# Three input loads of a dilated convolution, each in two transfers of half the rows

## The chip, the cores and the metric

The kernel runs on one core of a Trainium2 chip. The metric is the device time of one execution in microseconds. Beside it stands a profile of one execution, whose span reaches from the first instruction to the last.

## What is computed

A 3x3 convolution with dilation 2 and zero padding of 2, in float32, on 16 images of 64 channels and 64x64 points, with 128 output channels:

```python
batch, c_in, h, w, c_out, k, dilation = 16, 64, 64, 64, 128, 3, 2
...
x_pad = np.pad(x, ((0, 0), (0, 0), (pad, pad), (pad, pad)), mode='constant')
...
output[b, co] += weight[co, ci, kh, kw] * x_pad[b, ci, kh*dilation:kh*dilation+h, kw*dilation:kw*dilation+w]
```

The input has 16.8 MB and the output 33.6 MB.

## The kernel before

**Tiles.** Two images make a pair: their 2 x 64 channels fill the 128 partitions, so that one pair of input is 128 rows of 16 KB in HBM, one for each partition. There are eight pairs (`NP`), numbered from 0; the sixth to eighth are pairs 5, 6 and 7. A pair's output is a tile `o` of 128 partitions (output channels) by two images of 16 KB each, 4 MB in all.

**Arithmetic.** Input is held in float16 (`x16`, six buffers). Rows that stand two apart share part of their work: GpSimd (POOL in the profile) adds them to `s16` (three buffers, `prepare`, line 141), TensorE (PE) multiplies the sums once with the middle row of the weights (`w1`), and two more phases use differences of weight rows (`w21`, `w01`) and the outer rows. For each of four stretches `u` of 16 image rows, ScalarE (ACT) copies the first phase from PSUM to `s32` (line 204), and VectorE (DVE) adds it to the other two and writes `o` (line 209). The matmuls of the two images of a pair, 64 partitions each, are issued in turn (line 186).

**Loads.** Pair 0 comes as float32 by two transfers of SyncE's queue (SP, line 75), 36 and 28 rows, and is cast on chip. Pairs 1 to 7 come by `load` (lines 78 to 81): GpSimd issues the transfers, and they cast from float32 to float16 on the way. `load(pb, cuts)` makes one transfer for each stretch of rows between two neighbours in `cuts`. Pair 1 is issued among the preparation of the weights, pairs 2 to 4 after the first sum of pair 0 (`AHEAD` is 5). Pairs 5, 6 and 7 are issued in the main loop (line 196), at `u == 1` of pairs 3, 4 and 5, each ahead of `prepare` of the pair after that one (lines 199 and 201: rows 0 to 35, then the rest).

**What sets the order.** The schedule is by hand: each engine works off its instructions in the program's order and waits where it needs a result or a free buffer. GpSimd has little to do, so it runs ahead in the program until it needs a buffer: `prepare` of pair 4 waits for PE to be done with the `s16` of pair 1, and so on. So the loads of pairs 5 to 7 are issued long before PE comes to the place where they stand. The buffers of pairs 6 and 7 are those of pairs 0 and 1.

**Stores.** SP issues one store of 4 MB after each of pairs 0 to 4 (line 221), two of 2 MB (one per image) after pairs 5 and 6, and for pair 7 two of 1 MB after each half of its rows (line 224). Tile `o` has three buffers. Loads of GpSimd run in queue q0, all transfers of SP in queue q1; both are served by the same 16 DMA engines. A transfer over 128 partitions puts 8 partitions on each engine. A packet is one stretch of memory of one partition, 16 KB for a whole input row or one image of a store; each engine ends its part of a transfer with a small semaphore packet of 4 bytes.

Of the kernel before, what the change touches and what calls it, by code (L numbers as in the profile page):

```python
# [10 lines left out]
def kernel(  # L11
# [9 lines left out]
    B, CI, H, W = x.shape  # L21
# [56 lines left out]
    def load(pb, cuts):  # L78
        x16[pb] = x16pool.tile([P, H, W], f16, tag="x16", name=f"x16_{pb}")
        for lo, hi in zip(cuts, cuts[1:]):  # L80
            nc.gpsimd.dma_start(out=x16[pb][:, lo:hi], in_=x_pair[pb, :, lo:hi])  # L81
# [53 lines left out]
    def prepare(pb, lo, hi):  # L135
        if pb not in s16:
            s16[pb] = sumpool.tile([P, 2 * NQ, W], f16, tag="s16", name=f"s16_{pb}")
        src = (x16[pb] if pb else x32).rearrange("p (q e r) w -> p q e (r w)", e=2, r=2)
        dst = s16[pb].rearrange("p (q r) w -> p q (r w)", r=2)
        q0, q1 = lo // 4, hi // 4  # L140
        nc.gpsimd.tensor_add(  # L141
            out=dst[:, q0:q1], in0=src[:, q0:q1, 0, :], in1=src[:, q0:q1, 1, :]
        )
# [37 lines left out]
    def phase(pb, u, terms):  # L181

        ps = cpool.tile([CO, 2, NB], f32, tag="ps", name="ps")
        for pair in zip(*(conv(pb, hb, ps[:, hb], u, terms) for hb in range(2))):
            for m in pair:
                nc.tensor.matmul(**m)  # L186
        return ps

    BOTH = NP - 3
    for pb in range(NP):  # L190
        o = opool.tile([P, 2, H, W], f32, tag="o", name=f"o{pb}")
        ov = o.rearrange("p b (q e r) w -> p b q e (r w)", e=2, r=2)
        for u in range(NU):

            if u == 1 and AHEAD <= pb + 2 < NP:
                load(pb + 2, [0, H])
            if pb + 1 < NP:
                if u == 1:
                    prepare(pb + 1, 0, 36)
                elif u == 2:  # L200
                    prepare(pb + 1, 36, H)

            s32 = spool.tile([P, 2, NB], f32, tag="s32", name="s32")
            nc.scalar.copy(out=s32, in_=phase(pb, u, [("w1", 2, 0)]))  # L204
            for e, terms in enumerate(
                ([("w21", 1, 0), ("w0", 1, -1)], [("w01", 0, 0), ("w2", 0, 1)])
            ):
                ps = phase(pb, u, terms)
                nc.vector.tensor_add(  # L209
                    out=ov[:, :, u * UQ : (u + 1) * UQ, e, :],  # L210
                    in0=ps.rearrange("p b (q c) -> p b q c", c=QW),
                    in1=s32.rearrange("p b (q c) -> p b q c", c=QW),
                )

            step = NU // 2 if pb == NP - 1 else NU
            if (u + 1) % step == 0:
                fl = slice((u + 1 - step) * 4 * UQ, (u + 1) * 4 * UQ)
                if pb < BOTH:  # L220
                    nc.sync.dma_start(out=out_pair[pb], in_=o)
                else:
                    for hb in range(2):
                        nc.sync.dma_start(out=out[2 * pb + hb, :, fl], in_=o[:, hb, fl])
# [35 lines left out]
```

## Time and profile before

| what | value |
|---|---|
| median of 3 runs | 126.64 us (126.33 to 126.74) |
| profiled execution: span of its instructions | 124.3 us |
| busy: PE, DVE, POOL, ACT | 105.2, 80.8, 41.4, 39.6 us |
| read from and written to HBM | 17.07 and 33.55 MB, 407 GB/s over the span |
| queue q1 (SP: weights, pair 0, all stores) | 2944 packets, 68.9% of 16 engines' span |
| queue q0 (POOL: loads of pairs 1 to 7) | 1008 packets, 28.4% |
| load of one pair, issue to landing | 16.0 us in the median of 7 |
| store of 4 MB, issue to landing | 21.6 us in the median of 5 |

The profiled execution has no time of its own beside its span. Busy times are unions of an engine's instructions. In the table of 40 slices each digit is the busy share of one fortieth of the span in tenths, 9 for 90% or more; the DMA row is the mean over the 16 DMA engines, and the GB/s row counts what packets wrote, so a load that casts counts with half of what it read. The share of a queue is the time of its packets over 16 engines' time; since records of neighbouring packets overlap a little, the shares of a full stretch come to slightly over 100%. In a timeline row stand the start and the length of a run of like instructions, and in square brackets how long the engine was idle ahead of it and what ended that.

### The profile page before, as it was taken

What the parts mean: (1) busy time and instruction counts of PE and PEld (TensorE: products, weight loads), DVE (VectorE), ACT (ScalarE), POOL (GpSimd) and SP (SyncE); (2) the same over time, 40 slices, a digit from 0 to 9 for tenths busy, and PEclk for the clock granted to TensorE, in tenths of its full rate; (3) what the DMA queues carried; (4) which work ended last, traced back from release to release, by engine and by line L of the source; (5) the groups of instructions that cost most, each with busy time, mean ns of one, the idle gap of its engine ahead of it and who ended that gap; (6) DMA issues with size and microseconds to landing.
All of it is one profiled execution on the core that took longest, in us unless ns stands there. A gap on an engine that the chain in (4) does not pass through costs nothing.

```text
span 124.3 us, 2244 instructions
## 1 busy us (share of the span) xinstructions
PE 105.2 (85%) x981; PEld 55.7 (45%) x981; DVE 80.8 (65%) x71; ACT 39.6 (32%) x40; POOL 41.4 (33%) x33
## 2 busy tenths in 40 slices
PE   6357999999999999999999999999999999960000
PEld 2043555555555555555555555555555555520000
DVE  0470199787778777877769778777877787770000
ACT  4760823333333333333333333333332433320000
POOL 2859998794095009500930093000000000000000
PEclk9999999999999999999999999999999999999655
DMA  4999999999999999999999999999999999999991
GB/s 129 346 359 218 214 214 216 224 237 411 393 327 314 332 306 319 316 390 314 324 345 427 425 427 432 422 427 427 432 438 427 432 414 432 427 417 419 422 406 71
DMA packets 3961, 43.42 MB, mean 349 GB/s; under 512 B 368, under 2 KB 368, under 8 KB 624
## 3 DMA queue, kind: packets, MB, share of 16 engines
q1 hardware_dynamic: 2944, 35.95, 68.9%
q0 software_dynamic: 1008, 7.34, 28.4%
q8 instruction: 7, 0.11, 0.3%
q14 instruction: 2, 0.02, 0.0%
HBM read 17.07 MB, written 33.55 MB: 407 GB/s over the span
## 4 chain that ended last, share of the span: by engine, by line
PE 80%; DMA 5%; POOL 2%; DVE 1%; DVEq 1%; SPq 0%; issue 0%
PE ps L186 80%; DMA x<-in_x_dram 5%; POOL s L141 2%; DVE o L209 1%; DVEq L255 1%; SPq L64 0%; DVEq L209 0%
## 5 line engine op out<-in xcount | busy, mean ns | idle before, releaser
L209 DVE TENSOR_TENSOR o<-ps,s 128x1024 f32<-128x1024 f32 x64 | 76.7, 1223 | 25.9 <-PE ps L186 16.8
L186 PE MATMUL ps<-x,w_sb 64*128 64x496 f16 (+3 forms) x768 | 85.3, 368 | 0.0
L186 PEld LDWEIGHTS <-w_sb 64*128 64x128 f16 x960 | 53.4, 95 | 49.3 <-issue 3.7
L204 ACT COPY s<-ps 128x1024 f32<-128x1024 f32 x32 | 32.4, 1012 | 63.0 <-PE ps L186 63.0
L141 POOL TENSOR_TENSOR s<-x 128x1152 f16<-128x1152 f16 (+4 forms) x18 | 35.1, 1971 | 31.1 <-PE ps L186 28.3
L186 PE MATMUL ps<-s,w_sb 64*128 64x496 f16 (+1 forms) x192 | 26.5, 379 | 2.1 <-POOL s L141 2.1
L81 POOL DMA_DIRECT2D x<-in_x_dram x7 | 4.0, 579 | 0.0
L132 ACT CAST x<-x 128x1024 f16<-128x1024 f32 (+1 forms) x3 | 2.8, 973 | 3.4 <-DMA x<-in_x_dram 3.4
L93 PE MATMUL warm<-zero 128*128 128x512 f16 x6 | 2.7, 630 | 1.2 <-DVE zero L87 1.2
L117 PE MATMUL wt<-ident,w 128*128 128x128 f16 x15 | 1.8, 312 | 2.1 <-ACT w L99 2.1
L103 DVE TENSOR_TENSOR w<-w 128x192 f16<-128x192 f32 x2 | 1.5, 800 | 2.5 <-DMA w<-in_weight_dram 2.5
L117 PEld LDWEIGHTS <-w 128*128 128x128 f16 x15 | 1.5, 146 | 3.0 <-ACT w L99 3.0
L99 ACT CAST w<-w 128x576 f16<-128x576 f32 x2 | 2.3, 1222 | 1.6 <-DMA w<-in_weight_dram 1.6
L103 POOL TENSOR_TENSOR w<-w 128x192 f16<-128x192 f32 x2 | 1.9, 951 | 2.4 <-DMA w<-in_weight_dram 2.4
L126 DVE CAST w_sb<-wt 128x384 f16<-128x384 f32 x3 | 1.6, 552 | 1.4 <-PE wt L117 1.4
L93 PEld LDWEIGHTS <-zero 128*128 128x128 f16 x6 | 0.7, 138 | 2.3 <-DVE zero L87 1.2
L99 ACT ACT_TABLE_LOAD x1 | 1.3, 1283 | 0.7 <-PEq L241 0.7
L128 ACT CAST w_sb<-wt 128x384 f16<-128x384 f32 x2 | 1.0, 478 | 1.1 <-PE wt L117 1.1
L130 DVE CAST x<-x 128x1280 f16<-128x1280 f32 x1 | 0.8, 826 | 0.5 <-DMA x<-in_x_dram 0.5
L87 DVE MEMSET zero<- 128x256 uint32 x1 | 0.3, 272 | 0.9 <-PEq L241 0.9
masks.py:199 POOL TENSOR_SCALAR_AFFINE_SELECT ident<-ident 128x128 f16<-128x128 f16 x1 | 0.3, 292 | 0.1
masks.py:197 POOL MEMSET ident<- 128x128 f16 x1 | 0.2, 204 | 0.3 <-POOLq L241 0.3
(4 smaller groups left out, 0.4 us busy)
## 6 DMA issues: line engine op xcount, KB each, us to landing
out_dram<-o SPq DMA_DIRECT2D x5, 4096.0 KB, 21.6
out_dram<-o SPq DMA_DIRECT2D x4, 2048.0 KB, 12.4
x<-in_x_dram POOLq DMA_DIRECT2D x7, 1024.0 KB, 16.0
out_dram<-o SPq DMA_DIRECT2D x4, 1024.0 KB, 10.6
x<-in_x_dram SPq DMA_DIRECT2D x1, 1152.0 KB, 6.5
x<-in_x_dram SPq DMA_DIRECT2D x1, 896.0 KB, 10.6
w<-in_weight_dram SPq DMA_DIRECT2D x1, 288.0 KB, 2.9
```

Source lines behind the costliest of these rows:

```text
L81: nc.gpsimd.dma_start(out=x16[pb][:, lo:hi], in_=x_pair[pb, :, lo:hi])
L93: nc.tensor.matmul(out=warm[:, 0], lhsT=zero[:, 0:P], rhs=zero, start=True, stop=True)
L99: nc.scalar.copy(out=w16[:, 0:NK, u, :], in_=w32k)
L103: eng.tensor_sub(out=w16[:, SLOT[name] * KW : (SLOT[name] + 1) * KW, u, :], in0=w32k[:, a * KW : (a + 1) * KW, :], in1=w32k[:, KW : 2 * KW ...
L117: nc.tensor.matmul(out=ps[:, 0, j * CO : (j + 1) * CO], lhsT=w16[:, k0 + j, :, :].rearrange("o t i -> o (t i)"), rhs=ident, start=True, st ...
L126: nc.vector.tensor_copy(out=dst, in_=ps[:, 0, 0 : KW * CO])
L132: nc.scalar.copy(out=x16[0][:, lo:hi], in_=x32[:, lo:hi])
L141: nc.gpsimd.tensor_add(out=dst[:, q0:q1], in0=src[:, q0:q1, 0, :], in1=src[:, q0:q1, 1, :])
L186: nc.tensor.matmul(**m)
L204: nc.scalar.copy(out=s32, in_=phase(pb, u, [("w1", 2, 0)]))
L209: nc.vector.tensor_add(out=ov[:, :, u * UQ : (u + 1) * UQ, e, :], in0=ps.rearrange("p b (q c) -> p b q c", c=QW), in1=s32.rearrange("p b ( ...
L255: with _tile.TileContext(nc) as tc:
```

## The change

Where the loads of pairs 5, 6 and 7 are issued, the list of cuts gets 32 as a middle point, so each load becomes two transfers, of rows 0 to 31 and of rows 32 to 63. Each is still one stretch per partition, of 8 KB instead of 16 KB in HBM, and of 4 KB instead of 8 KB on chip. The tile, the casting and the place in the program stay. The loads of pairs 0 to 4 and all stores are as before.

```diff
             if u == 1 and AHEAD <= pb + 2 < NP:
-                load(pb + 2, [0, H])
+                load(pb + 2, [0, 32, H])
             if pb + 1 < NP:
                 if u == 1:
                     prepare(pb + 1, 0, 36)
```

## The prediction

> **What bounds the kernel now.** I read the page's slices first, then the chain of work, then the DMA view of single stretches, and last the packet records in order of their start.
>
> ```profile
> PE   6357999999999999999999999999999999960000
> ...
> DMA  4999999999999999999999999999999999999991
> GB/s 129 346 359 218 214 214 216 224 237 411 393 327 314 332 306 319 316 390 314 324 345 427 425 427 432 422 427 427 432 438 427 432 414 432 427 417 419 422 406 71
> ```
>
> The DMA engines are full from the second slice to the last but one. PE stops in the 36th slice, and three slices of nothing but transfers follow. GB/s counts a cast load by what it writes, half of what it reads, so the lower numbers in slices 4 to 9 and 12 to 21 are loads, not idle engines.
>
> ```profile
> PE ps L186 80%; DMA x<-in_x_dram 5%; POOL s L141 2%; DVE o L209 1%; DVEq L255 1%; SPq L64 0%; DVEq L209 0%
> ...
> 110.88 1.13 DVEq L255
> ```
>
> The chain names PE for 80% and ends at 112.0 us, 12 us before the span's end. It follows instructions; the rest of the span is the queue of transfers that it does not walk. The packet records show that queue: the last data packets end between 120.5 us on the engine done first and 122.9 us on the engine done last. PE's last matmul is at 110.3 us and the last store is issued at 112.4 us, while that store's first packet starts at 118.0 us. So the store had to wait for the queue, and **the end is the sum of all packets on the latest engine**; a cost on PE, DVE, ACT or POOL shows only when it makes that queue run empty.
>
> Does the sum close? On the engine done first, the fourth load's semaphore packet is at 27.68 us and its last at 120.54 us: 92.86 us. Five stores of 4 MB at 9.72 us, four of 2 MB at 4.86 and four of 1 MB at 2.455 make 77.9, three loads at 4.87 make 14.6, together 92.5 (the durations are distances between such packets of transfers that follow each other with nothing between). 0.36 us is left over, in the 24 places where loads and stores alternate.
>
> **The change, part by part.** The loads of pairs 5, 6 and 7 (image rows 0 to 31, then 32 to 63) become six transfers. Nothing else is edited.
>
> *Packets.* Each engine moves 8 partitions of a pair, in 8 packets of 16 KB read and 8 KB written. It will have 16 packets of 8 KB read and 4 KB written: 24 more packets per engine in all. The trace has no cast packet of that size. The nearest rows are stores of the two sizes:
>
> ```profile
> DMA packets 157, 2.57 MB, mean 429 GB/s; under 512 B 0, under 2 KB 0, under 8 KB 0
> ...
> q1 hardware_dynamic: 157, 2.57, 100.7%
> ...
> DMA packets 353, 2.57 MB, mean 429 GB/s; under 512 B 39, under 2 KB 39, under 8 KB 39
> ...
> q1 hardware_dynamic: 353, 2.57, 101.5%
> ```
>
> These are the stretches 74 to 80 us (16 KB stores) and 113.5 to 119.5 us (8 KB stores, 314 of them and 39 semaphore packets): the same bytes in the same 6 us. Finer, by semaphore packets: eight 16 KB packets take 4.86 us, two transfers of eight 8 KB packets 2 x 2.455 = 4.91, so +0.05 us for what one load becomes, with the added semaphore packet in it. Three loads: **+0.15 us**. A semaphore packet of POOL's queue takes 22 ns, not 9 as on SP's: 3 x 13 ns, **+0.04**. Lower bound nothing: no smaller packet in this trace moves bytes faster (7 KB packets of the second pair-0 load start every 268 ns, 26.7 B/ns; the 16 KB ones run at 27.0). Upper bound from the cast packets alone, below: their records fill 102.9% of the time, so of each one's 625 ns about 17 overlap the next; if a half packet pays that again in full, 24 x 17 ns = 0.41 us. I take 0.19, since the copy of 8 KB is the nearest row.
>
> *Alternation.* This is the term that I think is missed by looking at sizes alone.
>
> ```profile
> DMA packets 404, 3.01 MB, mean 215 GB/s; under 512 B 37, under 2 KB 37, under 8 KB 37
> ...
> q0 software_dynamic: 403, 3.00, 102.9%
> ...
> DMA packets 526, 6.09 MB, mean 321 GB/s; under 512 B 34, under 2 KB 34, under 8 KB 34
> ...
> q1 hardware_dynamic: 266, 4.10, 51.4%
> q0 software_dynamic: 258, 1.97, 49.5%
> ```
>
> The first pair of lines is 13.5 to 27.5 us, loads alone; the rest is 34 to 53 us, loads beside stores, in about equal number: one of each in turn. Engine time per data packet: loads alone (14 x 16 - 0.95 for one instruction fetch) / 366 = 609 ns; stores alone, from 74 to 80 us, 96 / 157 = 611 ns; mixed (19 x 16 - 2 x 0.95) / 490 = 616.5 ns. So a mixed packet costs 6 ns more, a load and a store together 12 ns. That agrees with the 0.36 us left over in the sum: 24 turns of 12 to 15 ns. With half packets there are 48 turns in place of 24: **+0.29 us**. Lower bound nothing (if the 12 ns belong to bytes, not to turns); upper bound twice that, 0.58, since the two windows cut packets at their edges.
>
> The Trainium skill (DMA: Bandwidth & Descriptors, "Queues, rings and completion order") says that an engine drains a whole packet of some 9 to 17 descriptors from one ring before it turns to the next. If a load's eight rows were such a packet, more rows would not mean more turns and this term would be nothing (rival B). The records speak against it: the sixth pair's load has its first packet at 33.3 us and its first engine done at 42.3, 9.0 us, where eight rows in succession take 4.87.
>
> *POOL.* Three more DMA issues, 0.57 us each as in the rows below, and waits that come later.
>
> ```profile
> 28.77 0.57 POOL L81 DMA_DIRECT2D x<-in_x_dram  x1
> 34.21 4.20 POOL L141 TENSOR_TENSOR s<-x 128x1152 f16<-128x1152 f16 x2 [4.86 <-PE ps L186]
> 38.36 0.57 POOL L81 DMA_DIRECT2D x<-in_x_dram  x1
> 46.58 4.21 POOL L141 TENSOR_TENSOR s<-x 128x1152 f16<-128x1152 f16 x2 [7.65 <-PE ps L186]
> 50.73 0.57 POOL L81 DMA_DIRECT2D x<-in_x_dram  x1
> 58.95 4.21 POOL L141 TENSOR_TENSOR s<-x 128x1152 f16<-128x1152 f16 x2 [7.65 <-PE ps L186]
> 71.31 4.21 POOL L141 TENSOR_TENSOR s<-x 128x1152 f16<-128x1152 f16 x2 [8.14 <-PE ps L186]
> ```
>
> The issues lie in front of POOL's idle 4.9 to 8.1 us: hidden. The landings move more. Beside stores, 16 half packets and 16 stores take 16 x (0.31 + 0.61) = 14.7 us where 8 and 8 took 9.8. So the sixth pair lands 4.9 us later (45.5 to 50.4 on the latest engine). prepare(5) sums rows 0 to 35, needs both halves, and starts at 50.4, not 46.58; it ends at 54.6, and load(7), behind it in POOL's program, is issued some 4 us later. The three loads then follow each other without a gap: the seventh pair lands near 65.5, the eighth near 79, prepare(7) ends near 83.5. PE takes pairs 5, 6 and 7 up at 74, 86.5 and 99 us (the issues of stores at 25.45, 37.82, 50.19, 62.56, 74.93, 87.30 and 99.75 mark the pairs' ends). Cover of 19, 16 and 15 us: cost nothing; past it, PE would wait microsecond for microsecond.
>
> *Does the queue run empty?* Stores get two thirds of the engines instead of half while loads run, so stores 0 to 2 end earlier: near 39.7, 54.4 and 69.0 instead of 41.7, 59.0 and 71.8 us. The next store's issues are at 37.82, 50.19 and 62.56, so it is there; where it is a little late, half packets of the load fill in. After the loads' end near 77 us the queue of stores is as long as before. DVE's one wait for a store (1.23 us at 62.5) goes; DVE had its result early enough that PE never waited for it, so nothing is won.
>
> **Sum.** 0.15 + 0.04 + 0.29 = +0.48 us on every engine, so on the latest too: span 124.3 to 124.8. The profiled execution has no time of its own beside its span; 126.64 - 124.3 = 2.3 us lie outside it and stay. 126.64 + 0.48 = **127.1 us**, +0.38%.
>
> **Rivals.**
>
> *B, no difference that can be told (0.42).* A measurement of this kernel can tell about 0.3% (0.38 us, up to 127.02) from no change; the three runs span 0.41 us. If turns cost nothing, 0.19 is left: 126.83. For it: 429 GB/s at both sizes. Against it: 616.5 against 610 ns. It decides where a turn costs under 8 ns.
>
> *C, each transfer has a price on the engines (0.06).* Last packet to landing is 0.35 us (42.33 to 42.68). If an engine stood still that long per added transfer: 3 x 0.35 + 0.48 = +1.5, 128.2. Against it: two 2 MB stores in succession, 2 x 4.86 us, take as long as one of 4 MB, 9.72. The Trainium skill speaks against this change most here (DMA: Bandwidth & Descriptors, "Anatomy of one DMA" and "Rules for kernel authors"): about 2.0 us fixed for each transfer, and at least 1 MiB each. By it three more cost 6 us, an estimate of 132.6, where nothing covers them; these rows show the cover, a queue that is never empty.
>
> *D, PE waits for a late pair (0.03).* It needs landings 15 us later than worked out; then each further microsecond that empties the queue adds one: 128 and up.
>
> *E, faster (0.06).* The latest engine ends 0.2 us after the next one, and seven instruction fetches of 0.95 us fall on single engines. If the changed program's fetches fell elsewhere, and turns came cheaper by bytes (-0.29), the end would come 0.2 + 0.29 - 0.19 = 0.3 us earlier: 126.3. Nothing in the trace asks for it.
>
> **Chances and range.** Forecast 0.43, B 0.42, C 0.06, D 0.03, E 0.06. Faster 0.06, same 0.42, slower 0.52. The range goes from 126.45 (no cost, and a median low in its spread) to 127.65 (0.41 + 0.07 for three semaphore packets + 0.58 = +1.06, rounded): C, D and the end of E are left out.
>
> **What would show it.** Queue q0 with 1440 packets instead of 1008; prepares of pairs 5 to 7 at about 50, 65 and 79 us, ended by a DMA; PE ending at 110 as before; no wait of DVE for out_dram; the first engine done near 121.0, not 120.54. Wrong: DMA slices under 9 between 40 and 110 us (C or D), a PE wait for POOL beyond the 2.1 us at the start (D), a mixed stretch with no more lost time than before (B).

## The result, and the profile after

The changed kernel takes **127.08 us** (126.73 to 127.5, 10 runs), the kernel before 126.66 us (126.33 to 127.04, 10 runs): +0.42 us, a ratio of 1.0039 with a 95% interval of 1.0020 to 1.0058. Its profiled execution has a span of 125.0 us, where the one of before has 124.3. Here and below, medians and ratios leave out runs that took over 1.5% more than the fastest run of the same kernel (three of the six with quarters, two of the six with one queue and whole loads, single ones elsewhere).

From the page of the changed kernel, the slices and the DMA queues:

```profile
DMA  4999999999999999999999999999999999999991
GB/s 132 353 356 215 212 215 215 218 191 414 415 349 339 356 341 377 350 377 331 369 346 364 350 347 377 419 414 419 430 430 435 432 435 419 425 419 419 425 388 68
DMA packets 4393, 43.42 MB, mean 347 GB/s; under 512 B 416, under 2 KB 416, under 8 KB 1440
...
q1 hardware_dynamic: 2944, 35.95, 68.8%
q0 software_dynamic: 1440, 7.34, 28.9%
```

The engines are as full as before. The stretch of loads beside stores reaches from the 12th to the 25th slice instead of the 12th to the 21st, with more stores in it (331 to 377 GB/s, where nine of the ten slices before had 306 to 345). Queue q0 moves the same 7.34 MB in 1440 packets instead of 1008.

The end of the chain of work, and POOL's timeline:

```profile
109.59 1.13 DVEq L255
```

```profile
50.31 4.21 POOL L141 TENSOR_TENSOR s<-x 128x1152 f16<-128x1152 f16 x2 [12.13 <-DMA x<-in_x_dram]
54.46 1.11 POOL L81 DMA_DIRECT2D x<-in_x_dram  x2
65.98 4.21 POOL L141 TENSOR_TENSOR s<-x 128x1152 f16<-128x1152 f16 x2 [10.42 <-DMA x<-in_x_dram]
81.35 4.21 POOL L141 TENSOR_TENSOR s<-x 128x1152 f16<-128x1152 f16 x2 [11.15 <-DMA x<-in_x_dram]
```

Work ends 1.3 us earlier than before (109.6 + 1.1 against 110.9 + 1.1), and the span is 0.7 us longer: the time is in the queue behind the work. (The 1.3 us come from the start, as told below.) The sums of pairs 5, 6 and 7 (rows 1, 3 and 4) now start when their data lands, at 50.3, 66.0 and 81.4 us. From the list of waits (microseconds in all, times, longest):

```profile
POOL s L141 <- DMA x<-in_x_dram: 37.1, 7, 12.1
...
PE ps L186 <- POOL s L141: 0.7, 1, 0.7
```

POOL waits 37 us for loads instead of 2.8, and PE waits for POOL only once, 0.7 us at the start. DVE's wait for a store is gone from the list.

One difference has nothing to do with loads 5 to 7. Stretch by stretch, of before and then of the changed kernel (columns: length, busy time and instructions of PE, PEld, DVE, ACT, POOL, granted clock, DMA share, GB/s):

```profile
24.00:28.00 4.00, 4.00 (x44) 2.12 (x41) 3.50 (x4) 1.21 (x2) 3.39 (x2) 1.00 1.06 240
```

```profile
24.00:28.00 4.00, 4.00 (x44) 2.09 (x40) 2.75 (x4) 1.52 (x2) 3.03 (x2) 1.00 1.02 199
```

Both move the fourth whole load here (215 GB/s is a load alone, so the 240 of before holds some store packets). In the changed kernel's execution 26 load packets between 25 and 29 us take 640 to 1139 ns instead of 625, 0.34 us for each engine. GpSimd's first sum ran ahead of VectorE's cast at 7.0 us, PE started at 8.6 us instead of 9.95, and the first store was issued at 24.2 instead of 25.45 us. Why load packets are late with this early start isn't seen: the store's own packets begin only at 28.0 us, no earlier than in the kernel before (27.7 us). So the extra span of this one execution can't be put down to the half packets alone.

### The profile page after: what moved, and what is told of

It reads as the page before. It is cut to its first block, busy times and chain, and to the rows that moved or that the text cites. A ratio compares the mean times of both kernels' runs of the same rounds, so it can differ in the third digit from the quotient of the medians.

```text
span 125.0 us, 2250 instructions
## 1 busy us (share of the span) xinstructions
PE 105.3 (84%) x981; PEld 54.3 (43%) x981; DVE 82.2 (66%) x71; ACT 39.6 (32%) x40; POOL 42.8 (34%) x36
## 2 busy tenths in 40 slices
DMA packets 4393, 43.42 MB, mean 347 GB/s; under 512 B 416, under 2 KB 416, under 8 KB 1440
## 3 DMA queue, kind: packets, MB, share of 16 engines
q0 software_dynamic: 1440, 7.34, 28.9%
## 4 chain that ended last, share of the span: by engine, by line
PE 80%; DMA 5%; POOL 1%; DVE 1%; DVEq 1%; SPq 0%; issue 0%
PE ps L186 80%; DMA x<-in_x_dram 5%; POOL s L141 1%; DVE o L209 1%; DVEq L255 1%; SPq L64 0%; DVEq L209 0%
## 5 line engine op out<-in xcount | busy, mean ns | idle before, releaser
L186 PEld LDWEIGHTS <-w_sb 64*128 64x128 f16 x960 | 52.1, 95 | 49.3 <-issue 2.4
L141 POOL TENSOR_TENSOR s<-x 128x1152 f16<-128x1152 f16 (+4 forms) x18 | 34.5, 1937 | 39.8 <-DMA x<-in_x_dram 37.1
L81 POOL DMA_DIRECT2D x<-in_x_dram x10 | 6.0, 600 | 0.0
L130 DVE CAST x<-x 128x1280 f16<-128x1280 f32 x1 | 2.1, 2133 | 0.0
```

Of the source, the lines that this page charges most:

```text
L130: nc.vector.tensor_copy(out=x16[0][:, 0:20], in_=x32[:, 0:20])
L141: nc.gpsimd.tensor_add(out=dst[:, q0:q1], in0=src[:, q0:q1, 0, :], in1=src[:, q0:q1, 1, :])
```

## The experiments

Theory T ("turn theory"): each turn of an engine from a load packet to a store packet and back costs a fixed time, and a half packet otherwise nearly half of a whole one. Rivals: a fixed cost of each cast packet even without stores (P, "packet theory"), a price of each transfer (C), the late landing (D), and, once the traces were seen, the start.

**Early halves.** Loads 1 to 4 in halves, where no store runs.

```diff
-                load(1, [0, H])
+                load(1, [0, 32, H])
...
-        load(pb, [0, H])
+        load(pb, [0, 32, H])
```

> The kernel before, but the loads of pairs 1 to 4 come by two transfers of 32 rows, those of pairs 5 to 7 whole: 32 more cast packets on each engine, nearly all in a stretch where no store runs beside them. Turn theory (each change of an engine between a load packet and a store packet costs 12 to 16 ns, size nearly nothing): eight half packets alone take 2.45 us and a pair 4.91 instead of 4.87, so about +0.2 us, 126.9 us. Packet theory (each cast packet costs some 16 ns beyond its bytes, with or without a store beside it): eight half packets alone take 2.50 to 2.56 us, a pair 5.0 to 5.1, so +0.5 to +0.9 us, 127.2 to 127.6 us.

Measured: 126.45 against 126.26 us, ratio 1.0013 (0.9992 to 1.0033); the interval ends at +0.42 us, below what P asks for. The DMA view of 11 to 27 us:

```profile
DMA packets 931, 3.42 MB, mean 214 GB/s; under 512 B 100, under 2 KB 100, under 8 KB 930
...
q0 software_dynamic: 930, 3.40, 105.9%
q8 instruction: 1, 0.02, 0.4%
```

930 - 100 = 830 half packets in (16 x 16 - 0.95) us of engine time are 307 ns each; a whole one alone is 609. So halving costs 2 x 307 - 609 = 5 to 6 ns per pair of halves, the added semaphore packet included, 0.05 us per load, and P falls: its eight halves would have taken 2.50 us or more, and the semaphore packets stand 2.46 us apart.

**Quarters.** Loads 5 to 7 in four transfers of 16 rows.

```diff
-                load(pb + 2, [0, H])
+                load(pb + 2, [0, 16, 32, 48, H])
```

> Pairs 5 to 7 by four transfers of 16 rows each: 72 more load packets on each engine than before, where the changed kernel has 24 more. Turn theory and packet theory both: three times the +0.42 us of the changed kernel, +1.2 to +1.3 us, 127.9 us, with PE ending as before and the loads landing later still. If the cost goes by bytes and not by packets, it stays at +0.4 us, 127.1 us. If late landings start to count (POOL's prepare of pair 7 past 95 us), PE waits for POOL and the time is above 128.5 us.

Measured: ratio 1.0167 (1.0127 to 1.0207), some 128.4 us, from three runs. POOL's timeline and the list of waits:

```profile
75.62 2.37 POOL L141 TENSOR_TENSOR s<-x 128x1152 f16<-128x1152 f16 x1 [15.73 <-DMA x<-in_x_dram]
81.71 1.88 POOL L141 TENSOR_TENSOR s<-x 128x896 f16<-128x896 f16 x1 [3.72 <-DMA x<-in_x_dram]
100.95 2.36 POOL L141 TENSOR_TENSOR s<-x 128x1152 f16<-128x1152 f16 x1 [17.36 <-DMA x<-in_x_dram]
107.04 1.88 POOL L141 TENSOR_TENSOR s<-x 128x896 f16<-128x896 f16 x1 [3.73 <-DMA x<-in_x_dram]
```

```profile
PE ps L186 <- POOL s L141: 6.7, 2, 4.5
```

The cover is used up: pair 7's sums start at 101 and 107 us, and PE stands still. Rival D is real, one halving further on: one quarter packet for each store packet gives a load only a fifth of an engine while stores are waiting (157 of 157 + 611 ns, by the figures below). The total is not a price per packet alone, since this stall is in it.

The turn itself can be read from the packet records of the mixed stretches: engine time less fetches and less 611 ns for each store, divided by the load packets, packets on an edge counted in part.

```
load packet       alone     beside stores             more
whole, 16 KB      609 ns    614 to 617 (2 executions) 5 to 8 ns
half, 8 KB        307 ns    315 to 317 (3 executions) 8 to 10 ns
quarter, 4 KB     157 ns    164                       7 ns
```

The quarter alone was not measured; it is an estimate, extended from the two sizes above it. The added time doesn't shrink with the packet, as it would if it went by bytes: T holds, with a turn of about 8 ns, where 12 to 16 were expected. 24 turns make 0.2 us. That the turns go row by row is seen in the counts; of the changed kernel from 34 to 53 us:

```profile
DMA packets 702, 6.72 MB, mean 354 GB/s; under 512 B 48, under 2 KB 48, under 8 KB 373
...
q1 hardware_dynamic: 344, 5.37, 67.6%
q0 software_dynamic: 357, 1.33, 34.6%
```

Without the 48 semaphore packets (16 in q1, 32 in q0) these are 328 store packets of a whole row and 325 load packets of half a row; the kernel before had 250 and 240 in the same time.

**Partition halves and quarters.** More transfers, the same data packets. The halves were also measured with another cast, told further down.

```diff
-                load(pb + 2, [0, H])
+                load_parts(pb + 2)
...
+        for p in (0, CI):
+            nc.gpsimd.dma_start(out=x16[pb][p : p + CI], in_=x_pair[pb, p : p + CI])
```

> Pairs 5 to 7 by two transfers each as in the changed kernel, but of 64 partitions with whole rows of 16 KB instead of 128 partitions with half rows: three more transfers, three more semaphore packets on each engine, and not one data packet or turn more. Turn and packet theory: +0.04 us, 126.7 us. If each transfer has a price of its own (0.42 us / 3 = 0.14 us): 127.1 us as the changed kernel.

> Two queues as before; pairs 5 to 7 by four transfers of 32 partitions each, whole rows: nine more transfers than before, the same data packets and turns. The partition halves measured +0.4 us in their medians, twice, while their traced executions show no added time on the DMA engines. If each added transfer has a price (0.14 us), three times that: +1.2 us, 127.6 us, and the trace must show where. If the partition halves' difference is one of the start or of chance: +0.1 us (nine semaphore packets of 13 ns), 126.5 us.

Measured: halves 126.72 against 126.26 us, 1.0033 (1.0021 to 1.0045), which is the number that C expects; quarters, with nine added transfers, 126.5 against 126.29, 1.0025 (1.0006 to 1.0044), which is T's. A price of 0.14 us per transfer falls with that, since nine would have made 1.2 us. In the traced execution of the quarters POOL issues four times in a row and the sums start as they did before:

```profile
38.22 1.99 POOL L86 DMA_DIRECT2D x<-in_x_dram  x4
46.43 4.21 POOL L146 TENSOR_TENSOR s<-x 128x1152 f16<-128x1152 f16 x2 [6.22 <-PE ps L191]
```

**Late whole loads.** `load(pb + 2, [0, H])` stands at `u == 3`, behind both sums.

```diff
-            if u == 1 and AHEAD <= pb + 2 < NP:
-                load(pb + 2, [0, H])
...
+            if u == 3 and AHEAD <= pb + 2 < NP:
+                load(pb + 2, [0, H])
```

> Whole loads as before, but pairs 5 to 7 are issued at u == 3, behind both sums of the next pair, so that each is issued some 6 to 12 us later and POOL's sums start about as late as in the changed kernel or later. No packet and no turn is added. Turn and packet theory: no change, 126.66 us. If the late landing is what costs in the changed kernel: 127.1 us or above, with a wait of PE for POOL.

Measured: 127.96 us, 1.0126 (1.0101 to 1.0151). My expectation was wrong, but not by a wait of PE for POOL:

```profile
28.00:36.00 8.00, 8.00 (x78) 4.07 (x76) 5.76 (x6) 3.04 (x3) 2.24 (x2) 1.00 1.00 423
36.00:39.00 3.00, 3.00 (x34) 1.72 (x32) 2.40 (x3) 1.01 (x1) 3.00 (x3) 1.00 0.55 235
39.00:41.00 2.00, 2.00 (x23) 0.97 (x19) 2.00 (x2) 0.39 (x1) 0.37 (x1) 1.00 0.95 393
```

From 36 to 39 us the engines are busy 55% of the time (the last column but one): on the first engine the first store is done at 37.3 us, the second is issued at 38.3 and load 5 at 38.8 us. About 1.4 us of engine time are lost there and never made up. Packets of the second store that are late (up to 1229 ns) cost each engine 0.9 us more between 40 and 47 us; this execution was the slowest of the six (128.56 us). So the loads of the kernel before fill a hole between stores 0 and 1; the changed kernel issues them at the same place and keeps it filled.

**The start taken out.** The cast of the first 20 rows on ScalarE, so that VectorE and GpSimd don't meet; with whole loads, halves, and partition halves.

```diff
-            nc.vector.tensor_copy(out=x16[0][:, 0:20], in_=x32[:, 0:20])
+            nc.scalar.copy(out=x16[0][:, 0:20], in_=x32[:, 0:20])
```

> Whole loads as before, but ScalarE instead of VectorE casts the first 20 rows of pair 0, so that VectorE and GpSimd don't touch the same tile at 7 us. In the traces so far the start has two courses: GpSimd's first sum ahead of VectorE's cast (PE starts at 8.6 us, the first store is issued at 24.2 us and meets the fourth load, whose last packets take 800 to 1500 ns: some 0.3 to 0.4 us on each engine) or beside it (PE at 9.5 to 10, first store at 25.2 to 26 us, nothing lost). The changed kernel and the partition halves were profiled in the first course, the kernel before in the second. Expected of this reference for the next two kernels: PE starts near 8.6 us and the time is that of the kernel before plus 0 to 0.4 us.

> The changed kernel with the same cast on ScalarE; to be compared with the one above, which has whole loads. Turn theory: +0.5 us over it (24 more turns of 15 ns, and 0.05 us per load for the half packets). If the +0.42 us of the changed kernel came from its start alone, no difference.

> Two transfers of 64 partitions with whole rows for each of pairs 5 to 7, with the cast on ScalarE; to be compared with the whole loads with that cast. Turn theory, with the start as the reason for the +0.46 us that the partition halves showed: +0.04 us. If a transfer has a price of its own, +0.4 us.

Measured on one chip, medians of 12: whole 126.26, halves 126.60, partition halves 126.69 us (ratios to the kernel before 0.9987, 1.0019 and 1.0022, each give or take 0.0016 to 0.0023). The halves keep +0.34 us with the start taken out; resampling the twelve runs of each gives a 95% interval of 0.03 to 0.55 us, so it is only just clear of noise. The partition halves again stand 0.4 us over the whole loads, which T does not explain, and the medians can't tell them from the row halves (0.09 us apart, -0.15 to 0.33).

**The changed kernel once more.**

> The changed kernel once more, to see which course its start takes and whether the difference holds on this chip: +0.42 us over the kernel before, as measured; in a trace with the second course of the start, packets alone would give +0.5 us.

Measured: 126.65 against 126.39 us, 1.0013 (0.9994 to 1.0032). This execution took the other start (VectorE's cast ahead of GpSimd's sum, PE at 9.5 us, first store issued at 25.65 us), and nothing is lost there:

```profile
24.00:28.00 4.00, 4.00 (x44) 2.16 (x42) 3.50 (x4) 1.02 (x2) 3.45 (x2) 1.00 1.04 233
```

Its span is 124.3 us, as in the kernel before: its first engine is done 0.48 us later (121.02 against 120.54 us), its latest at 122.9 as there. So single spans don't show the change. From the packet records, the time from the semaphore packets of a load to the last ones of all, as a mean over the 16 engines:

```
                                                  from pair 4's load    from pair 3's load
whole loads:        before                        93.33 us              98.33 us
                    early halves                  93.32
                    cast on ScalarE               93.39                 98.32
                    longer GpSimd program (below) 93.50                 98.45
row halves:         changed, again                93.81                 98.67
                    cast on ScalarE               93.72                 98.73
                    changed, first (early start)  93.26                 98.99
partition halves:   cast on ScalarE               93.40                 98.34
                    first (early start)           93.20                 98.75
partition quarters:                               93.58                 98.53
```

The two executions with the early start have their late load packets ahead of pair 4's landing, so that only the second column holds them. In that column row halves without late packets are 0.2 to 0.4 us above whole loads, and partition halves are among them. The early start adds some 0.3 us to the row halves and 0.4 us to the partition halves: in the first traced execution of the partition halves the added time is there, and it is the start's. Executions with whole loads scatter by 0.1 to 0.2 us.

**A longer GpSimd program.** Three small fills behind the three issues.

```diff
                 load(pb + 2, [0, H])
+                nc.gpsimd.memset(idle, 0.0)
```

> The kernel before with whole loads and no added transfer; behind each of the issues of pairs 5 to 7 GpSimd fills a small tile that nobody reads (some 0.5 us each), so that its program has three more instructions of about the length of an issue. If the +0.2 to +0.46 us that the partition halves and quarters measured without any added packet time come from GpSimd's longer program, this shows +0.2 to +0.4 us, too. If they come from the transfers, or from chance, no change: 126.3 us where the kernel before has 126.3.

Measured: 126.55 against 126.42 us, 1.0009 (0.998 to 1.0038): inconclusive, since the interval holds both no change and +0.4 us.

**One queue.** GpSimd issues the stores of pairs 0 to 3, and loads 5 to 7 stand two pairs earlier.

```diff
-            if u == 1 and AHEAD <= pb + 2 < NP:
-                load(pb + 2, [0, H])
+            if u == 1 and AHEAD <= pb + 4 < NP:
+                load(pb + 4, [0, H])
...
-                    nc.sync.dma_start(out=out_pair[pb], in_=o)
+                    (nc.gpsimd if pb < 4 else nc.sync).dma_start(out=out_pair[pb], in_=o)
```

> Whole loads, but GpSimd issues the stores of pairs 0 to 3, so that loads and these stores stand in one queue one behind the other and an engine does not change between them packet by packet. Since a store in GpSimd's program holds back what is behind it, the loads of pairs 5 to 7 are issued two pairs earlier (at u == 1 of pairs 1 to 3; pairs 6 and 7 still find their buffers free). Turn theory: the 24 turns of about 15 ns go, -0.3 to -0.4 us against the kernel before, 126.0 us, as long as the queue never runs empty. Without a price of a turn: no change.

> The same one queue with loads 5 to 7 in halves of 32 rows; to be compared with the one-queue kernel with whole loads. Turn theory: only the half packets are left of the changed kernel's cost, +0.15 to +0.2 us. If the cost belongs to the half packets or to the transfers themselves: +0.4 to +0.5 us.

Measured: 129.1 us with whole loads, 1.0234 (1.0196 to 1.0272), and 129.12 us with halves, 1.0219 (1.0201 to 1.0237). Loads and stores no longer take turns, and the time is 2.8 us longer, where T expected a gain; the two can't be told apart, and each loses time in its own way, so this says nothing of a turn or of the halves. Part of the reason, with whole loads, from the same columns as above:

```profile
34.00:37.00 3.00, 3.00 (x32) 1.61 (x30) 2.25 (x3) 1.01 (x1) 0.00 (x0) 1.00 1.03 415
37.00:40.00 3.00, 3.00 (x32) 1.61 (x30) 2.40 (x3) 1.01 (x1) 1.38 (x3) 1.00 0.96 216
40.00:43.00 3.00, 3.00 (x32) 1.52 (x30) 2.28 (x3) 1.01 (x1) 3.00 (x2) 1.00 1.05 158
```

From 40 to 43 us the engines are full and move loads alone, at 158 GB/s where a load alone moved 215 before. The packet records name the packets behind it: between 34 and 60 us those that are late (over 640 ns) add 1.8 us to each engine, 1.2 us of it in load packets, against 0.04 in the kernel before. With halves the engines also stand idle for a while: they are busy 90% from 102 to 104 us and 45% from 104 to 106 us.

## Why the prediction was right

The predicted 127.1 us and the direction hold against the first measurement, +0.42 us. The three comparisons of row halves with whole loads gave +0.42, +0.34 and +0.26 us, and their mean of 0.34 is less than the forecast's +0.48, so that the closeness of the first is in part luck. By the prediction's own steps:

- **The bound** was the packet queue. In the first execution work ended 1.3 us earlier and the span became longer, and the changed kernel's PE waits for nothing after the start. "On every engine, so on the latest too" does not show in one span: the latest engine of the second execution ended as before.
- **Packets, +0.15 us, and semaphore packets, +0.04:** confirmed by half packets alone (307 against 609 ns): 24 x 2 x 307 - 24 x 609 ns = 0.12 us, or 0.05 us per load, 0.15 us for three. The added semaphore packets of POOL's queue are in this, so that the +0.04 on top of it does not show. The nearest row, stores of 8 KB, was the right one, and the upper bound of 17 ns per packet is excluded.
- **Alternation, +0.29 us:** the mechanism held, and the size was too high: about 8 ns per turn, not 12, so 0.2 us. The stretch of 34 to 53 us had cut packets at its edges; with these counted in part, its mean is 614 ns, not 616.5. The 0.36 us left over in the sum was no check on the turns, since late packets and fetches were not taken out: as a mean over the 16 engines some 0.85 us are left over, of which six instruction fetches make 0.36 and late store packets after 34 us some 0.2 us. What remains is some 0.25 us for 24 turns. Sum of the terms as measured: 0.3 to 0.4 us.
- **Turns row by row:** the counts of packets and the duration of the loads fit one load packet to one store packet. The rule of the Trainium skill by which the turns would not have grown (DMA: Bandwidth & Descriptors, "Queues, rings and completion order": a whole packet of descriptors before an engine turns) is not borne out here.
- **Landings:** the sums of pairs 5, 6 and 7 were forecast to start at 50, 65 and 79 us; they started at 50.3, 66.0 and 81.4 us, the last 2.4 us late and still with cover. PE never waited for them. That the cover was finite, and where it ends, is shown by the quarters.
- **Does the queue run empty?** It did not, as forecast, and the late whole loads show how near that was: moved behind the sums, the same loads left the engines idle 45% of 3 us.
- **Not foreseen:** the two courses of the start. In the first execution of the changed kernel late load packets held each engine up, and counted from pair 3's load some 0.3 us of that is left at the end. The forecast of the first engine's end, 121.0 us, was met by the second execution of the changed kernel (121.0), and missed by the first (121.3), which had the early start.
- **Rivals:** B is not excluded by the repeated measurement (its interval includes no change), only by the first one and the packet records together; and with 8 ns the turn lies on B's own border. C's price per transfer is excluded at 0.14 us. Open stays why the medians of the partition halves were 0.4 us up, twice. The first traced execution of them has its added time in the early start; the one with the cast on ScalarE shows next to nothing (98.34 against 98.32 us), but it was the fastest of its kernel's twelve (126.23 us), so what the slower ones did is not seen. As long as that is open, the medians alone don't show that the changed kernel's time went into half packets and turns: something that comes with any split of a load would explain them as well. The packet records show it, in two executions of row halves beside three of whole loads. No version here beats the kernel before.

## What to carry to other kernels

Where the DMA engines are never idle, as here, the time is the sum of their packets, and the chain of instructions that a profile prints ends before the story does: look for the gap between the last store's issue and its first packet. Cutting its rows then cost per packet and per turn with the other queue, a few nanoseconds each, and it also slowed that stream in favour of the other; the second effect was free until PE had to wait for the data. Before moving a load, ask which hole between stores it fills.

## What the runs showed of the hardware

- A load packet between stores costs about 8 ns more than in a row of loads, at 16 and at 8 KB (at 4 KB 7 ns, against an estimate of the row alone); two half packets in a row of loads cost 5 to 6 ns more than a whole one.
- The share of an engine that a stream gets beside another goes by packets: one load packet to one store packet, so quarters made a load last over 20 us where whole rows took 9.
- Stores and loads in one queue were not cheaper in the form tried here (129.1 against 126.3 us, with the loads also issued two pairs earlier). Where the queue went from stores to loads (37 to 43 us in the one-queue fence), packets that take 611 to 625 ns elsewhere took up to 1521.
- The same program starts in two ways. Where GpSimd's sum starts ahead of VectorE's cast (7.01 and 7.09 us in the first execution of the changed kernel), the sum takes 1.54 us and the cast 2.13 us; where the cast is ahead (7.18, and the sum at 7.23 us, in the second), they take 2.17 and 0.83 us. It isn't the tile that they share: with ScalarE casting the same rows of the same tile (6.91 us) beside GpSimd's sum (6.96 us), the sum takes 1.54 us.
